# An encoder trunk of two layers: GpSimd's tensor work goes to VectorE, with wider table products and another interleaving

## Chip, cores and metric

The kernel runs on one core of a Trainium2 chip. The metric is the device time of one execution in microseconds (us). The core has five engines that run their own queues of instructions in order: PE (TensorE, matrix products), DVE (VectorE), ACT (ScalarE), POOL (GpSimd) and SP (SyncE, which only issues transfers here). SBUF is the working memory, PSUM the memory that PE writes.

## What is computed

Two layers over 512 tokens of width 1024, all in float32. Each layer is a mixer with two halves, an output projection, a layer norm, an MLP and a second layer norm:

```
h = layer_norm(x)
for each layer:
    proj = h @ w_in                       # z 1024 | x, B, C 2048 | dt 32 | u 1024
    xbc  = silu(depthwise_conv(xbc, 5 taps))
    y_ssd = rms_norm((scan_forward + scan_backward + D * x) * silu(z))    # 16 heads, 4 groups, chunks of 128
    y5 = Re(C s) + d * u                  # S5: 64 groups, complex diagonal state, forward and backward scans
    y_s5 = rms_norm(g * sigmoid(g @ w_glu + b)),  g = gelu(y5)
    h = layer_norm(alpha * h + concat(y_ssd, y_s5) @ w_out)
    h = layer_norm(alpha * h + relu(h @ w1)**2 @ w2)
```

## The kernel before

**Matrix products.** Every float32 product is made of three products of a faster type: a weight tile `raw` is split into `whi` (a rounded copy, ACT, L98) and `wlo` = `raw` - `whi` (L99), the activations likewise, and `mm3` (L105 to L111) adds hi*hi, hi*lo and lo*hi. `proj_tile` (L123) gives 128 output channels for 512 tokens in 24 matmuls; `rows_proj` (L678) gives rows of tokens. The input projection has 32 such tiles in a layer (16 for x, B and C, named `xbc_ps`; 8 `u_ps`; 8 `z_ps`), the GLU 8 (`glu_ps`), the first MLP matrix 32 (`up_ps`); the output projections and the second MLP matrix are `rp`, of which the SSD half of the output projection is the first in a layer.

**The SSD half** (`ssd_group`, L566). For each group: two convolved tiles (`conv_tile`, L539: four taps on DVE, one of them in some tiles on ACT and POOL), B in rows, the products `CB`. For each pair of heads: the chunk states (`xd` L592, `S` L604), and for each head two scans `E2` and `E` (L620, L621), a weight `w` (eight ACT copies, L626 and L627, and a sum L628), the product `E` (L630) and two products `eb` (L631, L632), then the matmuls into `y_ps`.

**The S5 half** (`s5_stream`, L761) works in chunks of 8 tokens. u goes through DRAM (`Ud`). An input table for each of 8 batches and both directions (`s5_vtab`, L372; the tile `Wv` from the loaded `Pv` and `Bv`, six products and sums of 128x512 a direction, L385 to L387) feeds the matmuls `v_ps`, which fill `XV`. Then comes a recurrence of 62 steps over the chunks (`s5_scan`, L408, the tiles `sc`): four DVE instructions for each of two independent parts of 64 columns, L419, L420, L422 and L424, where L422 needs L420, L424 needs L422, and the next step needs L424. Then come output tables (`s5_wtab`, L426; the tile `Wy`, six instructions of 128x512 a direction, L461 to L463, and six small ones of 128x128 for `cp`), the small kernel `kk` that goes to DRAM (`KKd`) and comes back as `Gt`, and the outputs `y`, which are transposed into the GLU's input. For layer 0 the tables are made inside its mixer. For layer 1 they are made during the MLP of layer 0 (`s5_tables`, L491, a generator) and stored in DRAM.

**The MLP** (`mlp_up`, L896). For each `up_ps` tile: ACT takes Relu into `hr` (L903), POOL squares it (L904), ACT copies the rounded half `ahi` (L907), DVE subtracts for `alo` (L908). After each of the first 24 tiles a digit of the string `gen` says how many pieces of `s5_tables` are put into the program.

**What sets the order.** The program is written in one order, in which the lists `mrg` say how many pieces of `s5_stream` stand before each piece of `ssd_group`. A scheduler then reorders instructions on each engine by its own estimate of time and by priorities; the splits always have a raised one, and a table `po` shifts that of named pieces (`scan`, `w`, `v`, `z`, `dt`). Strings of letters (`wu`, `wx`, `wz`, `em`, `yz`, `ct`, `v0`, `v1`, `w0`, `w1`, `gv0` to `gw1`, `glu`, `ln0`) choose DVE (V), POOL (G) or ACT (S) for each instruction that several engines can do. Numbers of buffers limit how far loads and producers run ahead: `Bv` has one, `up_ps` two PSUM banks, `Wy` four (two batches).

Of the kernel before, what the change touches and what calls it, by code (L numbers as in the profile page):

```python
# [1037 lines left out]
```

## Time and profile before

| | before |
|---|---|
| time, median of 3 runs | 2099.39 us (2098.39 to 2099.54) |
| span of the profiled execution | 2094.1 us |
| PE busy | 1754.4 us (84%) |
| DVE busy | 1418.6 us (68%) |
| POOL busy | 837.1 us (40%) |
| ACT busy | 725.5 us (35%) |
| mean granted TensorE clock | 0.914 of full speed |

The profile is of one execution. Its span runs from the first to the last instruction; its own time is not listed apart from the span, and the median of the runs is 5.3 us above it, which is what lies around the span. Stages by the trace: layer 0's mixer to about 637 us, its GLU and projections to 729 us, its MLP to about 1197 us, layer 1's mixer to about 1638 us, its GLU and projections to 1730 us, its MLP to the end.

### The profile page before, as it was taken

To read this page: it belongs to the slowest core of one execution; us is meant where nothing else is said; L and a number is where in the kernel's file an instruction comes from. 1 tells how busy PE (TensorE), PEld (TensorE's weight loads), DVE (VectorE), ACT (ScalarE), POOL (GpSimd) and SP (SyncE) were. 2 spreads that over 40 slices of the span, in tenths; PEclk is the share of its full clock that TensorE was granted. 3 is DMA by queue.
4 is the path that set the end of the run, shared out by engine and by line. 5 is a ranking of instruction groups with operands and counts; after the bars stand their busy time and mean duration, and the time that the engine had idled before them with its cause. 6 is when DMAs were issued, how large, how long until landed. Compare 5 with 4: busy or idle time off the path is not lost.

```text
span 2094.1 us, 28322 instructions
## 1 busy us (share of the span) xinstructions
PE 1754.4 (84%) x10872; PEld 1427.8 (68%) x10872; DVE 1418.6 (68%) x2449; ACT 725.5 (35%) x1156; POOL 837.1 (40%) x557
## 2 busy tenths in 40 slices
PE   3677766676799995967899998776799999999998
PEld 3556555564578883745688887655677888888886
DVE  7468999999956767598733636999963564333335
ACT  2224433354215331211223336244563434232231
POOL 4456755445431128688702234344341112021121
PEclk8779887887799997979899999897999999999999
DMA  4655533434353355656533477542587233323232
GB/s 172 174 149 139 138 96 93 121 83 125 87 177 103 99 123 171 197 161 190 172 102 92 139 225 215 138 119 86 143 215 246 92 110 91 100 91 101 83 108 81
DMA packets 131239, 279.94 MB, mean 134 GB/s; under 512 B 12320, under 2 KB 58400, under 8 KB 130464
## 3 DMA queue, kind: packets, MB, share of 16 engines
q1 hardware_dynamic: 114144, 252.05, 41.8%
q10 hardware_dynamic: 16960, 26.09, 3.6%
q8 instruction: 85, 1.39, 0.3%
q14 instruction: 50, 0.41, 0.1%
HBM read 241.26 MB, written 36.83 MB: 133 GB/s over the span
## 4 chain that ended last, share of the span: by engine, by line
PE 44%; DVE 34%; DMA 9%; POOL 6%; issue 4%; ACT 1%; SPq 1%; POOLq 0%; DVEq 0%; ACTq 0%
PE rp L110 7%; PE rp L111 7%; PE rp L109 7%; PE up_ps L110 4%; PE up_ps L109 4%; PE up_ps L111 4%; DVE sc L422 4%; DVE XV L424 4%; DVE sc L420 4%; DVE sc L419 3%; DMA cb<-in_cb 3%; DMA Bv<-in_bb 2%; DVE E L620 2%; DVE E L621 1%; PE y L519 1%
## 5 line engine op out<-in xcount | busy, mean ns | idle before, releaser
L98 ACT ACTIVATE whi<-raw 128x1024 fp32r<-128x1024 f32 x224 | 236.2, 1057 | 494.9 <-PE rp L111 117.0
L99 DVE TENSOR_TENSOR wlo<-raw,whi 128x1024 fp32r<-128x1024 f32 x166 | 226.3, 1365 | 246.1 <-ACT whi L98 245.6
L904 POOL TENSOR_TENSOR hr<-hr 128x512 f32<-128x512 f32 x64 | 103.2, 1614 | 375.7 <-ACT hr L903 375.7
L99 POOL TENSOR_TENSOR wlo<-raw,whi 128x1024 fp32r<-128x1024 f32 x58 | 142.5, 2459 | 194.1 <-ACT whi L98 187.5
L109 PE MATMUL up_ps<-hThi,whi 128*128 128x512 f32 (+1 forms) x560 | 209.3, 376 | 3.5 <-ACT hr L903 3.2
L110 PE MATMUL up_ps<-hTlo,whi 128*128 128x512 f32 (+1 forms) x560 | 209.5, 375 | 0.1
L111 PE MATMUL up_ps<-hThi,wlo 128*128 128x512 f32 (+1 forms) x560 | 209.2, 374 | 0.0
L110 PE MATMUL rp<-wlo,ahi 128*128 128x512 f32 x448 | 184.0, 411 | 21.3 <-DVE wlo L99 21.3
L109 PE MATMUL rp<-whi,ahi 128*128 128x512 f32 x448 | 174.1, 410 | 21.5 <-ACT whi L98 13.1
L111 PE MATMUL rp<-whi,alo 128*128 128x512 f32 x448 | 182.8, 408 | 0.0
L109 PE MATMUL xbc_ps<-hThi,whi 128*128 128x512 f32 x256 | 113.6, 444 | 41.1 <-ACT z L649 23.6
L109 PEld LDWEIGHTS up_ps<-hThi,whi 128*128 128x128 f32 x560 | 105.9, 190 | 23.9 <-ACT hr L903 4.3
L111 PEld LDWEIGHTS up_ps<-hThi,wlo 128*128 128x128 f32 x560 | 106.4, 190 | 19.1 <-issue 0.4
L110 PEld LDWEIGHTS rp<-wlo,ahi 128*128 128x128 f32 x448 | 88.5, 197 | 44.8 <-DVE wlo L99 23.6
L110 PEld LDWEIGHTS up_ps<-hTlo,whi 128*128 128x128 f32 x560 | 106.3, 190 | 18.6 <-DVE hTlo L175 0.3
L109 PEld LDWEIGHTS rp<-whi,ahi 128*128 128x128 f32 x448 | 87.5, 196 | 43.8 <-ACT whi L98 14.4
L111 PE MATMUL xbc_ps<-hThi,wlo 128*128 128x512 f32 x256 | 111.2, 434 | 1.7 <-POOL wlo L99 1.7
L110 PE MATMUL xbc_ps<-hTlo,whi 128*128 128x512 f32 x256 | 111.4, 435 | 0.0
L908 DVE TENSOR_TENSOR alo<-hr,ahi 128x512 fp32r<-128x512 f32 x64 | 53.6, 839 | 76.6 <-ACT ahi L907 76.3
L111 PEld LDWEIGHTS rp<-whi,alo 128*128 128x128 f32 x448 | 88.3, 197 | 22.2
L422 DVE TENSOR_TENSOR sc<-sc,XV 128x64 f32<-128x64 f32 x248 | 101.9, 429 | 1.9
L420 DVE TENSOR_TENSOR sc<-XV,l 128x64 f32<-128x64 f32 x248 | 101.9, 411 | 0.0
(287 smaller groups left out, 4414.0 us busy)
## 6 DMA issues: line engine op xcount, KB each, us to landing
raw<-in_w SPq DMA_DIRECT2D x128, 512.0 KB
raw<-in_wi SPq DMA_DIRECT2D x64, 512.0 KB
Pv<-pd SPq DMA_DIRECT2D x32, 512.0 KB
ab<-ad SPq DMA_DIRECT2D x32, 512.0 KB
eb<-ad SPq DMA_DIRECT2D x32, 512.0 KB
raw<-in_wo SPq DMA_DIRECT2D x32, 512.0 KB
Bv<-in_bb SPq DMA_DIRECT2D x16, 512.0 KB
U<-Ud SPq DMA_DIRECT2D x128, 64.0 KB
```

What stands on the lines that cost most here:

```text
L98: S.activation(hi, raw, AF.Copy)
L99: e.tensor_tensor(lo, raw, hi.bitcast(F32), op=ALU.subtract)
L109: PE.matmul(o, lhsT=sh, rhs=mh, start=first, stop=False)
L110: PE.matmul(o, lhsT=sh, rhs=ml, start=False, stop=False)
L111: PE.matmul(o, lhsT=sl, rhs=mh, start=False, stop=last)
L419: V.tensor_tensor(t2[i], x[:, ::-1, hs[i]], l8[:, 1, :, hs[i]], op=ALU.mult)
L420: V.tensor_tensor(t1[i], x[:, :, hs[i]], l8[:, 0, :, hs[i]], op=ALU.mult)
L422: V.tensor_tensor(t1[i], t1[i], x1[:, :, hs[i]], op=ALU.add)
L424: V.tensor_tensor(x1[:, :, hs[i]], t1[i], t2[i], op=ALU.add)
L620: V.tensor_tensor_scan(E2, ab[:, 0], C("md"), NEG, op0=ALU.add, op1=ALU.max)
L904: G.tensor_tensor(r, r, r, op=ALU.mult)
L908: V.tensor_tensor(hl, r, hh.bitcast(F32), op=ALU.subtract)
```

## The change

Every tensor operation of POOL is now on DVE; POOL keeps the powers of -0.5 (L150, L673 before), which are one column or four wide. The strings that chose engines are gone. The input table of a direction is made by three instructions of 128x1024 where there were six of 128x512, for which ACT makes a negated copy of `Bv`; the output table likewise, from a copy `pw2` of the powers and a `cp` with a third part. The recurrence runs in one part of 128 columns. In the MLP ACT squares the Relu's result into `ahi` directly, and DVE computes max(`up_ps`, 0) * `hr` from PSUM. `xd` is read from PSUM instead of from the copied row. The `eb` loads take only the 384 columns in use. Fewer buffers for tables, other numbers in `mrg` and `gen`, other priorities.

```
-    wu=["GGGGGGGG", "VGGVGGGG"], wx=["GGGGGGGGGGGGGGGG", "GGGGGGGGGVGVGVGV"], wz=["GVGGGGGG", "GGGVGGGG"],
...
-    v1="GG", w0="VG", w1="GV", gv0="VG", gv1="GG", gw0="GV", gw1="VG", vb=(4, 2), gvb=(4, 3), cbb=2, wyb=4, raw=2,
-    whi=3, wlo=3, nb=dict(mm=3, ss=1, sm=2, s5=2), po=[{}, {"scan": -150, "w": -35}], glu="VVVVGVVV", ln0="SVSG",
-    sn=[2, 2], gen="110211101100201101103101",
+    vb=(3, 2), gvb=(3, 2), cbb=2, wyb=4, raw=2, whi=3, wlo=3, nb=dict(mm=3, ss=1, sm=2, s5=2),
+    po=[{"dt": 60, "scan": 300, "z": 30, "v": 60}, {"scan": -30, "w": -150}], sn=[1, 1], gen="110101122100001130301100",
...
-    def split(hi, lo, raw, e):
+    def split(hi, lo, raw):
         with tc.high_priority():
             S.activation(hi, raw, AF.Copy)
-            e.tensor_tensor(lo, raw, hi.bitcast(F32), op=ALU.subtract)
+            V.tensor_tensor(lo, raw, hi.bitcast(F32), op=ALU.subtract)
...
+        S.activation(B[:, 0], B[:, 2], AF.Copy, scale=-1.0)
...
-            for ri, e in enumerate((e0, e1)[dd]):
-                t1 = pool.tile([128, 512], F32, tag="tv%d" % (e is G), name="tv", bufs=1)
-                e.tensor_tensor(v4(W[:, ri]), P[:, :, 0], v4(B[:, ri]), op=ALU.mult)
-                e.tensor_tensor(v4(t1), P[:, :, 1], v4(B[:, 1 - ri]), op=ALU.mult)
-                e.tensor_tensor(W[:, ri], W[:, ri], t1, op=ALU.add if ri else ALU.subtract)
+            t1 = pool.tile([128, 2, 512], F32, tag="tv", name="tv", bufs=1)
+            pb = lambda r: P[:, :, r].unsqueeze(1).to_broadcast([128, 2, 4, 128])
+            V.tensor_tensor(v4(W), pb(0), v4(B[:, 1:3]), op=ALU.mult)
+            V.tensor_tensor(v4(t1), pb(1), v4(B[:, 0:2]), op=ALU.mult)
+            V.tensor_tensor(W, W, t1, op=ALU.add)
...
-            for ri, e in enumerate((e0, e1)[dd]):
-                t1 = pool.tile([128, 4, 8, 16], F32, tag="tw%d" % (e is G), name="tw", bufs=1)
-                e.tensor_tensor(w[:, ri], cpb(ri), pb(0), op=ALU.mult)
-                e.tensor_tensor(t1, cpb(1 - ri), pb(1), op=ALU.mult)
-                e.tensor_tensor(w[:, ri], w[:, ri], t1, op=ALU.subtract if ri else ALU.add)
+            V.tensor_tensor(wv, cpb(0), pb(0), op=ALU.mult)
+            V.tensor_tensor(t, cpb(1), pb(1), op=ALU.mult)
+            V.tensor_tensor(wv, wv, t, op=ALU.add)
...
-                G.tensor_tensor(xd, X[:, c0:c0 + 3].rearrange("p c (h q) -> p c h q", h=2),
+                V.tensor_tensor(xd, Xp[:, c0:c0 + 3].rearrange("p c (h q) -> p c h q", h=2),
...
-                G.tensor_tensor(w, w, w2, op=ALU.add)
+                V.tensor_tensor(w, w, w2, op=ALU.add)
...
-                G.tensor_tensor(eb[:, 0, 128:512], CT[:, 128:512], eb[:, 0, 128:512], op=ALU.mult)
-                G.tensor_tensor(eb[:, 1, 0:384], CT[:, 0:384], eb[:, 1, 0:384], op=ALU.mult)
+                V.tensor_tensor(eb[:, 0], CT[:, 128:512], eb[:, 0], op=ALU.mult)
+                V.tensor_tensor(eb[:, 1], CT[:, 0:384], eb[:, 1], op=ALU.mult)
...
                     S.activation(r, o, AF.Relu)
-                    G.tensor_tensor(r, r, r, op=ALU.mult)
...
-                    S.activation(hh, r, AF.Copy)
+                    S.activation(hh, r, AF.Square)
+                    V.scalar_tensor_tensor(r, o, 0.0, r, op0=ALU.max, op1=ALU.mult)
                     V.tensor_tensor(hl, r, hh.bitcast(F32), op=ALU.subtract)
```

The order of the instructions moves at many places. Two of them follow. The first is DVE's queue at the end of layer 0's mixer; `sc` and `XV` are the recurrence, `Wy` and `tw` the output tables, and `h_... <- rp` the four results of the first half of the SSD output projection. Before:

```order
L424 TENSOR_TENSOR XV<-sc_2901,sc_2903 128x2x16x2
L99 TENSOR_TENSOR wlo<-raw,whi 128x1024 x2
L461 TENSOR_TENSOR Wy<-cp,pw 128x512 x2
L463 TENSOR_TENSOR Wy<-Wy,tw 128x512
L672 TENSOR_SCALAR r_ssd<-rms_ps 128x4
L462 TENSOR_TENSOR tw<-cp,pw 128x512
L463 TENSOR_TENSOR Wy<-Wy,tw 128x512
L99 TENSOR_TENSOR wlo<-raw,whi 128x1024
L462 TENSOR_TENSOR tw<-cp,pw 128x512
L851 SCALAR_TENSOR_TENSOR h_4588<-rp_4941,r_ssd,h_4588 128x512
```

and now:

```order
L666 TENSOR_SCALAR r_ssd<-rms_ps 128x4
L417 TENSOR_TENSOR XV<-sc_1990,sc_1991 128x64x2
L412 TENSOR_TENSOR sc_2051<-XV,l_287 128x128
L413 TENSOR_TENSOR sc_2050<-XV,l_287 128x128
L415 TENSOR_TENSOR sc_2050<-sc_2050,XV 128x128
L845 SCALAR_TENSOR_TENSOR h_4257<-rp_4469,r_ssd,h_4257 128x512
L845 SCALAR_TENSOR_TENSOR h_4258<-rp_4470,r_ssd,h_4258 128x512
L417 TENSOR_TENSOR XV<-sc_2050,sc_2051 128x64x2
L845 SCALAR_TENSOR_TENSOR h_4259<-rp_4471,r_ssd,h_4259 128x512
```

Before, the recurrence of layer 0 is over when the SSD projection's first results come, and the last output tables stand beside them. Now 22 of the 62 steps stand behind the first of these results and 10 behind the last of all eight, and the output tables of six of the eight batches come after the recurrence. In layer 1 the recurrence now ends at the last of the eight results.

The second place is the MLP of layer 0. POOL's queue before (`hr` the squares, `Wv` and `tv`, `Wy` and `tw` the tables of layer 1):

```order
L904 TENSOR_TENSOR hr<-hr 128x512
L387 TENSOR_TENSOR Wv<-Wv,tv 128x512
L461 TENSOR_TENSOR Wy<-cp,pw 128x512
L462 TENSOR_TENSOR tw<-cp,pw 128x512
L461 TENSOR_TENSOR Wy<-cp,pw 128x512
L463 TENSOR_TENSOR Wy<-Wy,tw 128x512
L904 TENSOR_TENSOR hr<-hr 128x512
```

and DVE's queue now, where the tables, the square (`hr<-up_ps,hr`) and the splits stand in one line:

```order
L902 TENSOR_TENSOR alo<-hr,ahi 128x512
L378 TENSOR_TENSOR Wv<-Pv,Bv 128x1024
L379 TENSOR_TENSOR tv<-Pv,Bv 128x1024
L378 TENSOR_TENSOR Wv<-Pv,Bv 128x1024
L380 TENSOR_TENSOR Wv<-Wv,tv 128x1024
L93 TENSOR_TENSOR wlo<-raw,whi 128x1024
L435 TENSOR_TENSOR tc_6463<-cb,co 128x128
L436 TENSOR_TENSOR tc_6464<-cb,co 128x128
L901 SCALAR_TENSOR_TENSOR hr<-up_ps,hr 128x512
```

The square has moved from POOL to DVE, and up to seven other DVE instructions stand between one tile's `alo` and the next tile's square. POOL's whole queue now holds 24 small powers and the fills at the start and before each layer.

## Rows read from the trace of the kernel before

**Rows 1.** The page's first part, busy time, share and instructions by engine.

```profile
span 2094.1 us, 28322 instructions
PE 1754.4 (84%) x10872; PEld 1427.8 (68%) x10872; DVE 1418.6 (68%) x2449; ACT 725.5 (35%) x1156; POOL 837.1 (40%) x557
```

**Rows 2.** Windows: stretch, its length, busy time of five engines, granted clock, DMA share, GB/s.

```profile
55.00:188.00 133.00, 87.43 (x688) 70.03 (x688) 77.59 (x82) 39.15 (x71) 81.11 (x48) 0.81 0.61 158
188.00:460.00 272.00, 192.72 (x1239) 155.49 (x1239) 265.01 (x574) 102.08 (x187) 140.80 (x94) 0.83 0.42 109
460.00:594.00 134.00, 95.50 (x910) 73.26 (x906) 122.50 (x225) 51.69 (x92) 73.36 (x56) 0.82 0.42 127
...
760.00:1045.00 285.00, 218.22 (x1296) 170.41 (x1295) 211.35 (x198) 56.67 (x83) 215.86 (x138) 0.87 0.59 176
...
1200.00:1325.00 125.00, 111.69 (x1110) 94.94 (x1108) 73.23 (x163) 56.68 (x101) 49.15 (x30) 0.98 0.71 211
1325.00:1540.00 215.00, 162.09 (x969) 132.05 (x970) 208.72 (x538) 104.08 (x190) 87.02 (x64) 0.87 0.50 134
1540.00:1595.00 55.00, 52.96 (x548) 42.14 (x548) 19.30 (x30) 27.96 (x47) 20.14 (x18) 0.94 0.82 229
...
1750.00:2088.00 338.00, 335.64 (x1460) 273.65 (x1458) 129.83 (x150) 96.47 (x123) 52.48 (x34) 1.00 0.31 95
```

**Rows 3.** Timeline of POOL at 193 us: start, length, instruction, idle before it.

```profile
193.67 2.40 POOL L99 TENSOR_TENSOR wlo<-raw,whi 128x1024 fp32r<-128x1024 f32 x1 [6.46 <-ACT whi L98]
```

**Rows 4.** Timeline of DVE from 192 to 194 us.

```profile
192.19 0.27 DVE L419 TENSOR_TENSOR sc<-XV,l 128x64 f32<-128x64 f32 x1
192.37 0.26 DVE L420 TENSOR_TENSOR sc<-XV,l 128x64 f32<-128x64 f32 x1
192.66 0.28 DVE L422 TENSOR_TENSOR sc<-sc,XV 128x64 f32<-128x64 f32 x1
...
193.29 0.27 DVE L419 TENSOR_TENSOR sc<-XV,l 128x64 f32<-128x64 f32 x1
...
193.78 2.42 DVE L422 TENSOR_TENSOR sc<-sc,XV 128x64 f32<-128x64 f32 x1
```

**Rows 5.** The tile xbc: count, shortest, median and longest ns, first and last start.

```profile
L546 DVE SCALAR_TENSOR_TENSOR xbc<-xbc_ps,sp,xbc x32: 724/739/750, 130.4 to 1555.3; 128x511 f32<-128x511 f32 x32
```

**Rows 6.** Timeline of DVE at three places without POOL beside it.

```profile
235.73 0.68 DVE L385 TENSOR_TENSOR Wv<-Pv,Bv 128x512 f32<-128x512 f32 x1
236.33 0.68 DVE L386 TENSOR_TENSOR tv<-Pv,Bv 128x512 f32<-128x512 f32 x1
...
1352.37 1.22 DVE L99 TENSOR_TENSOR wlo<-raw,whi 128x1024 fp32r<-128x1024 f32 x1
1353.50 0.26 DVE L422 TENSOR_TENSOR sc<-sc,XV 128x64 f32<-128x64 f32 x1
...
1378.68 1.22 DVE L620 TENSOR_TENSOR_SCAN E<-ab,cst 128x512 f32<-128x512 f32 x1
```

**Rows 7.** Groups by line and shape, 0 to 600 us: busy, mean ns, idle before.

```profile
L424 DVE TENSOR_TENSOR XV<-sc,sc 128x64 f32<-128x64 f32 x124 | 55.8, 470 | 1.2
...
L620 DVE TENSOR_TENSOR_SCAN E<-ab,cst 128x512 f32<-128x512 f32 x16 | 25.9, 1616 | 1.2 <-DMA ab<-ad 1.2
...
L385 DVE TENSOR_TENSOR Wv<-Pv,Bv 128x512 f32<-128x512 f32 x16 | 20.0, 1256 | 34.2 <-DMA Bv<-in_bb 25.6 <-DMA Pv<-pd 8.6
...
L99 POOL TENSOR_TENSOR wlo<-raw,whi 128x1024 fp32r<-128x1024 f32 x31 | 76.9, 2483 | 86.6 <-ACT whi L98 84.6 <-DVE xbc L547 2.0
```

**Rows 8.** The same for 1197 to 1540 us.

```profile
L422 DVE TENSOR_TENSOR sc<-sc,XV 128x64 f32<-128x64 f32 x124 | 47.8, 408 | 0.8
...
L99 POOL TENSOR_TENSOR wlo<-raw,whi 128x1024 fp32r<-128x1024 f32 x23 | 56.1, 2438 | 81.8 <-ACT whi L98 77.2 <-DMA U<-Ud 4.6
```

**Rows 9.** Timeline of ACT: the first GLU result of layer 0 and of layer 1.

```profile
643.28 0.69 ACT L872 ACTIVATE sg<-glu_ps,sp 128x512 f32<-128x512 f32 x1 [3.54 <-PE glu_ps L111]
...
1645.75 0.69 ACT L872 ACTIVATE sg<-glu_ps,sp 128x512 f32<-128x512 f32 x1
```

More of the change, by code (lines that the diff above doesn't have):

```diff
@@ L128, in proj_tile, with proj_halves @@
         return o
-    def proj_halves(srcs, act, tag, name, es):
-        ws = [wunit(x, e) for x, e in zip(srcs, es)]
+    def proj_halves(srcs, act, tag, name):
+        ws = [wunit(x) for x in srcs]
         os_ = [psum(tag[i % len(tag)], name) for i in range(len(srcs))]
@@ L237, in params @@
         S.activation(cs, r, AF.Sin)
[L239 removed]
+        pw = pool.tile([128, 2, 2, 9, 32], F32, tag="pp_pw", name="pw", bufs=1)
         V.memset(pw[:, 0, :, 0, :], 1.0)
@@ L256, in params @@
             V.tensor_tensor(o[:, 1], ta[:, 1, :, 0:m], tb_[:, 1, :, 0:m], op=ALU.add)
+        pw2 = per.tile([128, 2, 2, 8, 8, 8], F32, tag="pw2", name="pw2", bufs=1)
+        for ri in range(2):
+            for dd in range(2):
+                for x in range(2):
+                    S.activation(pw2[:, ri, dd, :, :, 4 * x:4 * x + 4],
+                                 pw[:, ri, dd, 1:9].rearrange("p k (m q) -> p k m q", q=4), AF.Copy)
         pd = dr.tile([2, 8, 32, 2, 128], F32, tag="pd", name="pd", bufs=2)
@@ L294, in params @@
         V.tensor_tensor(co[:, 1], co[:, 1], den, op=ALU.mult)
-        return dict(P=P_, A=Acol, pw=pw, l8=l8, co=co, pd=pd)
+        return dict(P=P_, A=Acol, pw2=pw2, l8=l8, co=co, pd=pd)
     def dt_prep(l, pool, hT, prm):
@@ L615, in ssd_group @@
                 ab = pool.tile([128, 2, T], F32, tag="ab", name="ab", bufs=1)
-                eb = pool.tile([128, 2, T], F32, tag="eb", name="eb", bufs=2)
-                for i, x in enumerate((ab, eb)):
-                    nc.sync.dma_start(x,
-                                      dtp["ad"][:, hh, i].rearrange("d c s -> d (c s)").unsqueeze(0).to_broadcast([128, 2, T]))
+                eb = pool.tile([128, 2, 384], F32, tag="eb", name="eb", bufs=2)
+                nc.sync.dma_start(ab, dtp["ad"][:, hh, 0].rearrange("d c s -> d (c s)").unsqueeze(0).to_broadcast(
+                    [128, 2, T]))
+                for dd in range(2):
+                    nc.sync.dma_start(eb[:, dd], dtp["ad"][dd, hh, 1, 1 - dd:4 - dd].rearrange(
+                        "c s -> (c s)").unsqueeze(0).to_broadcast([128, 384]))
                 V.tensor_tensor_scan(E2, ab[:, 0], C("md"), NEG, op0=ALU.add, op1=ALU.max)
@@ L662, in rms_add @@
         if k == 0:
-            G.tensor_copy(ssq, sq)
+            V.tensor_copy(ssq, sq)
         else:
-            G.tensor_tensor(ssq, ssq, sq, op=ALU.add)
+            V.tensor_tensor(ssq, ssq, sq, op=ALU.add)
     def rms_end(ssq, name):
@@ L757 @@
         G.memset(XV[:, :, :, 0::127], 0.0)
-        os_ = proj_halves([A["wi"][l, 16 + m] for m in range(3)], act, ["mm"], "u_ps", ens(KN["wu"][l]))
+        os_ = proj_halves([A["wi"][l, 16 + m] for m in range(3)], act, ["mm"], "u_ps")
         with pool_("dt%d" % l) as pool:
@@ L897, in mlp_up @@
                 if q == 0:
-                    os_ = proj_halves([A["w1"][l, m] for m in range(3)], act, ["s5", "s5", "mm"], "up_ps", [V] * 3)
+                    os_ = proj_halves([A["w1"][l, m] for m in range(3)], act, ["s5", "s5", "mm"], "up_ps")
                 hid = []
```

102 lines of the change are left out of this document (43 added, 59 removed), and 4 rows, old and new, of the table mrg.

## The prediction

> **What bounds the kernel now.** I read the busy times first [rows 1]: PE leads with 1754.4 us, DVE has 1418.6 and POOL 837.1 of 2094.1. These are averages over unlike stages, so I went to the windows by stage [rows 2]. In the MLP of layer 1 (1750 to 2088 us) PE is busy for 335.6 of 338 us at full clock; nothing on DVE or POOL can shorten that. The same holds for the GLU and the projections of both layers. In layer 0's mixer the picture turns: from 188 to 460 us DVE is busy for 265 of 272 us, from 460 to 594 for 122.5 of 134, PE for seven tenths and at a clock of 0.83. From 1325 to 1540 us, layer 1's mixer, DVE has 208.7 of 215. From 760 to 1045 us, the MLP in which the next layer's tables are made, POOL has 215.9 and DVE 211.4 of 285, and PE 218.2 at 0.87. So three stages can give time: two mixers that DVE bounds and one MLP that waits for DVE and POOL in turn.
>
> The third view is the timeline, read for why DVE is so busy. An instruction of the recurrence on 64 columns takes 0.27 us; the same instruction at 193.78 us takes 2.42 us [rows 4], and POOL began a `wlo` of 2.40 us at 193.67 [rows 3]: they end 0.13 us apart. A DVE instruction with two SBUF operands stands still while POOL works on SBUF. One that reads PSUM does not: the 32 convolution taps of L546 lie between 724 and 750 ns wherever they stand [rows 5]. The group means show how much of DVE's busy time is such waiting: 470 ns for the 124 instructions of L424 in layer 0 and 1256 ns for L385 [rows 7], where free ones take 260 to 280 ns [rows 4] and 680 ns [rows 6].
>
> **The change part by part.** Prices first, from start to start of free neighbours: 0.60 us for two SBUF operands of 512 columns, 1.13 us for 1024 [rows 6], so 1.035 ns a column; hence 0.47 for 384 columns. A recurrence instruction of 64 columns takes 0.18 us behind an independent one [rows 4], so one of 128 takes 0.18 + 0.066 = 0.246.
>
> *Layer 0's mixer, stretch removed.* The four recurrence groups, of which one is shown [rows 7], hold 218 us in 496 instructions; free they are 496 x 0.26 = 129: 89 us. The six table groups, one shown [rows 7], hold 104 us in 93 instructions, free 93 x 0.68 = 63: 41. The two scans of each head, 32 instructions with 25.9 [rows 7] and 24.4 us, take 1.22 us free [rows 6]: 11. The smaller groups (coefficients, `E`, splits): 16. Together 157 us.
>
> *Added to DVE there.* 31 `wlo` [rows 7] x 1.13 = 35; POOL's 93 table instructions, which become half as many of twice the width, 93 x 0.565 = 53; 16 sums `w` x 0.60 = 10; 32 `eb` and 16 `xd` x 0.47 = 23; 16 others (`E`, gate, taps, sums of squares) x 0.62 = 10. Together 131 us.
>
> *Saved by width.* The recurrence: 62 x (8 x 0.18 - 4 x 0.246) = 28; DVE's own tables 93 x (0.60 - 0.565) = 3. So DVE needs 157 + 31 - 131 = 57 us less.
>
> *What is late next.* Before, the tables end at 600 us, where the stretch of rows 7 ends, and the first GLU result comes at 643.3 [rows 9]; between them PE still has some 90 of the SSD projection's 192 matmuls to do, 20 us at the 338 us in which layer 1's MLP does 1536 [rows 2]. Now the projection stands ahead of the outputs, under the recurrence's tail: 20 us off the end. Against that, `Wy` has room for two batches, so the third must wait for the first output, which needs the last step: 5 us. And ten steps stand behind the projection with nothing between them. A dependent pair starts 0.29 us apart and a step of 64 columns 1.10 [rows 4], so a step of 128 alone takes 1.10 + 4 x 0.066 = 1.36 and not 0.98: 4 us. DVE's 55 idle us from 55 to 188 [rows 2] are mostly waits for `Bv` and `Pv` (34 us at L385 [rows 7]). `Bv` has one buffer, and POOL, whose table instructions also queue behind `wlo` of 2.48 us [rows 7], gives it back late. I take 15 of the 55, between none and all. Layer 0: -57 - 20 - 15 + 5 + 4 = -83, with ends of -40 (the 57 less some 17 for waits that the rows don't show) and -130 (all 55 idle us gone).
>
> The VectorE page of the Trainium skill ("VectorE: DVE Perf Modes", The DRAIN you can't avoid) says that a chain of VectorE instructions pays the same gap with or without semaphores. By that the ten steps would lose nothing and the sum would be 4 us lower; the starts in the rows above show the dependent pair later, so I go by them.
>
> *Layer 0's MLP.* PE's 218.2 us at 0.87 are 190 at full clock, so at most 95 of the 285 us [rows 2] can go. The square leaves POOL, whose queue put it behind tables; ACT's square costs what its copy cost. DVE gets one instruction of about 0.74 us from PSUM [rows 5] for each tile. A piece of tables now takes DVE 6 x 1.13 = 6.8 us, or 8.5 with the seven small ones. In the first quarter DVE has 7 x 6.8, 8 tiles x (1.13 + 0.60 + 0.74), 14 us for the second matrix and about 70 small instructions x 0.26 for the parameters: 100 us, against PE's 84, a quarter of 338. In the third, 8 x 8.5 + 34 = 102. So 16 + 18 us stay lost, of which the second quarter takes 9 back, and I add 5 for waits at single tiles: -65, with ends of -30 and -95.
>
> The change adds a wait here: the PSUM bank of an `up_ps` tile was free after ACT's Relu and is now free after DVE's square. Behind that waits PE, two tiles on. I cost it at nothing, since a second bank covers one tile of about 5 us. With that cover gone, 24 tiles would lose 6.8 - 5.3 each, 36 us; that lies inside the ends.
>
> *Layer 1's mixer.* There are no tables. Stretch: the recurrence, one group shown [rows 8], 184 us - 129 = 55, scans and others 13. Added: 23 `wlo` [rows 8] x 1.13 = 26, `w`, `eb`, `xd` and others 37. Width: -28. DVE alone would end 33 us earlier, at 1507. PE may not follow. Its work from 1200 to 1595 is 112 x 0.98 + 162 x 0.87 + 53 x 0.94 = 300 us at full clock [rows 2]; the SSD projection's 41 come in, and the 320 output matmuls go behind (31 us at 53.0 us for 548 records [rows 2]). That makes 310. At a share of 0.93, between 0.89 and 0.96 in the first and the last of these stretches, it ends at 1533. Then come 31 us of outputs and 14 us for the last GELU, transposes, splits and the first GLU tile: 1578, where it was 1645.8 [rows 9]. That is -68, with ends of -33 (DVE's part alone) and -91 (PE without a gap).
>
> *At nothing:* the negated `Bv`, the copy `pw2` and the ACT square, since ACT has 35% [rows 1]; the layer norms' DVE form; the shorter `eb` loads; the sums of squares in the GLU stage, where PE bounds. If ACT were late, each of the 16 `Bv` copies would cost a table 0.6 us, 10 us in all.
>
> **Sum.** -83 - 65 - 68 = -216: a span of 2094.1 - 216 = 1878 us. The median of the runs lies 5.3 us over the span, so **1883 us**. The ends add up to -103 and -316: 1996 and 1783.
>
> **Rivals.**
> *The S5 tail lies bare* (chance 0.17). All six late output tables of layer 0 follow one another with the trip of `kk` through DRAM unhidden, 15 us more for each batch, a little more than the 9 us of one table: +90, so 1973 us. For it: the tail now stands behind the SSD half with no other work of PE beside it. Against it: `Wy` has four buffers, so a table can run beside the trip of the one before.
> *PE without gaps* (0.08). All upper ends hold and the clock stays at full: 1788 us. Against it: no mixer stretch shows it.
> *The stretch is not POOL's doing* (0.05), but that of transfers or of access patterns. Then 131 - 31 us are added in layer 0, 63 - 28 in layer 1, and DVE in layer 0's MLP gets 21 + 68 on top of 211 of 285, +15: 2099 + 150 = 2249 us, slower. It decides from where less than 6 tenths of the stretch goes away (100 of 157, 35 of 68). Against it stand the two instructions that end together at 196 us, and the taps from PSUM that are never stretched.
>
> The Trainium skill ("Perfetto Trace Analysis", Optimizing Scalar/DVE Operations) says that with a saturated VectorE it may make sense to move work to ScalarE or even GPSIMD, which speaks for the kernel before; by it this change would cost the 131 and 63 us that DVE takes on. The same paragraph warns of the read port that the two share, and the rows above bear the warning out.
>
> That the change does not do what it says is out: POOL's queue holds 24 small powers and a few fills.
>
> **How the numbers follow.** The forecast has 0.68, the three rivals 0.17, 0.08 and 0.05; 0.02 is left for no difference (within 0.2%, about what a measurement of this kernel can tell). Faster: 0.68 + 0.17 + 0.08 = 0.93; slower 0.05. The range of 1800 to 1990 us holds the forecast's ends nearly whole and the first rival.
>
> **What would show it.** Right: L424's successor at about 0.33 us for 128 columns and no two-operand instruction over 1.3 us; DVE's sum between 1230 and 1330 us in place of 1418.6; layer 0's first GLU result near 560, its MLP about 65 us shorter, layer 1's first GLU result 68 us nearer to the start of its mixer. Wrong: single stretched instructions without POOL; DVE idle before `Wy` between two batches; PE waiting for `hr` in layer 0's MLP; a clock that stays at 0.83 in the mixers.

## The result, and where the time went

Four runs of the changed kernel have a median of 2031.57 us (2027.98 to 2032.78), those of the kernel before beside them 2098.89: a ratio of 0.9689 (95% interval 0.9668 to 0.9710). It is faster by 67 us; the prediction said 1883 us, with a range from 1800 to 1990. The profiled execution has a span of 2029.3 us where the one before had 2094.1 [rows 1].

The first part of the page of the changed kernel answers to [rows 1]:

```profile
span 2029.3 us, 27508 instructions
PE 1738.4 (86%) x10872; PEld 1416.0 (70%) x10872; DVE 1342.7 (66%) x2300; ACT 728.1 (36%) x1175; POOL 33.6 (2%) x31
```

POOL is nearly empty, and VectorE's sum fell by 76 us although it took on POOL's work: the stretch is gone, as said, though 1342.7 is still 13 us over the top of what the prediction gave as a sign of being right (1230 to 1330). The time by stage, each boundary the first matmul of its kind in the trace, shows what did not follow (the last column is a run of the experiments, taken up there):

| stage, us | before | after | forecast change | measured | moved_only |
|---|---|---|---|---|---|
| start to layer 0's first GLU matmul | 637.0 | 621.8 | -83 | -15 | 595.3 |
| GLU and projections | 91.9 | 92.6 | 0 | +1 | 92.6 |
| layer 0's MLP, to layer 1's first `u` tile | 465.0 | 406.2 | -65 | -59 | 397.4 |
| layer 1's mixer, to its first GLU matmul | 444.0 | 451.2 | -68 | +7 | 431.1 |
| the rest | 456.3 | 457.6 | 0 | +1 | 459.9 |

The MLP came out as forecast; both mixers did not. The windows of the changed kernel, columns as in [rows 2], show where in them:

```profile
188.00:460.00 272.00, 204.88 (x1255) 168.62 (x1254) 243.30 (x479) 139.04 (x258) 0.00 (x0) 0.86 0.44 116
460.00:512.00 52.00, 30.01 (x125) 24.17 (x123) 47.64 (x115) 7.64 (x7) 1.05 (x1) 0.80 0.37 122
512.00:622.00 110.00, 74.72 (x1053) 55.99 (x1054) 50.16 (x70) 12.74 (x30) 0.00 (x0) 0.78 0.35 90
714.00:1120.00 406.00, 384.66 (x2159) 309.64 (x2158) 290.97 (x437) 123.97 (x181) 5.35 (x4) 0.97 0.54 169
...
1320.00:1490.00 170.00, 135.41 (x697) 111.69 (x696) 159.04 (x344) 86.63 (x153) 1.14 (x1) 0.91 0.39 118
1490.00:1572.00 82.00, 57.61 (x665) 43.51 (x666) 2.42 (x5) 10.29 (x18) 0.00 (x0) 0.82 0.72 188
```

Up to 512 us VectorE is busy for 243 of 272 and for 48 of 52 us, and then, for 110 us, no engine bounds: PE is busy for 75 of them, VectorE for 50, at a granted clock of 0.78. In layer 1 the same from 1490 to 1572: VectorE, busy for 159 of the 170 us before, has 2.4 of 82. These are the output tails of S5. What begins them stands in the timelines of VectorE and PE of the changed kernel (start, length, instruction, idle before it):

```profile
509.62 0.38 DVE L415 TENSOR_TENSOR sc<-sc,XV 128x128 f32<-128x128 f32 x1
510.03 0.37 DVE L417 TENSOR_TENSOR XV<-sc,sc 128x128 f32<-128x128 f32 x1
510.44 0.37 DVE L412 TENSOR_TENSOR sc<-XV,l 128x128 f32<-128x128 f32 x1
510.73 0.36 DVE L413 TENSOR_TENSOR sc<-XV,l 128x128 f32<-128x128 f32 x1
511.12 0.37 DVE L415 TENSOR_TENSOR sc<-sc,XV 128x128 f32<-128x128 f32 x1
511.53 0.37 DVE L417 TENSOR_TENSOR XV<-sc,sc 128x128 f32<-128x128 f32 x1
```

```profile
493.36 0.39 PE L105 MATMUL rp<-whi,hTlo 128*128 128x512 f32 x1
512.05 1.97 PE L515 MATMUL y<-Wy,XV 64*64 64x128 f32 x16 [18.30 <-DVE XV L417]
```

PE stands for 18.3 us and starts the first output when the last step of the recurrence has ended. In the kernel before, PE and VectorE stood like this:

```profile
457.80 1.09 PE L519 MATMUL y<-Wy,XV 64*64 64x128 f32 x16
```

```profile
577.58 1.35 DVE L424 TENSOR_TENSOR XV<-sc,sc 128x64 f32<-128x64 f32 x1
```

The first output ran 121 us **ahead** of the last step. With two parts, batches 0 to 3 need only the first part, which led by far; four of eight batches were through by 548 us, under the second part's steps, and three of layer 1's ahead of its last step at 1536. One part of all eight batches takes that away. The first GLU results, to be held against [rows 9] (the prediction had the one of layer 0 near 560 us), in ScalarE's timeline of the changed kernel:

```profile
632.92 0.69 ACT L866 ACTIVATE sg<-glu_ps,sp 128x512 f32<-128x512 f32 x1
...
1582.85 0.69 ACT L866 ACTIVATE sg<-glu_ps,sp 128x512 f32<-128x512 f32 x1
```

### The profile page after: what moved, and what is told of

It reads as the page before. It is cut to its first block, busy times and chain, and to the rows that moved or that the text cites. A ratio compares the mean times of both kernels' runs of the same rounds, so it can differ in the third digit from the quotient of the medians.

```text
span 2029.3 us, 27508 instructions
## 1 busy us (share of the span) xinstructions
PE 1738.4 (86%) x10872; PEld 1416.0 (70%) x10872; DVE 1342.7 (66%) x2300; ACT 728.1 (36%) x1175; POOL 33.6 (2%) x31
## 4 chain that ended last, share of the span: by engine, by line
PE 47%; DVE 24%; DMA 20%; issue 4%; ACT 3%; SPq 2%; POOLq 0%; POOL 0%; ACTq 0%; DVEq 0%
PE rp L103 6%; PE rp L105 6%; PE rp L104 6%; PE up_ps L103 5%; PE up_ps L104 5%; PE up_ps L105 5%; DMA ab<-ad 5%; DMA Bv<-in_bb 4%; DVE wlo L93 3%; PE y L515 3%; DMA Vd<-Wv 2%; PE glu_ps L103 1%; DMA raw<-in_wi 1%; PE glu_ps L104 1%; PE glu_ps L105 1%
## 5 line engine op out<-in xcount | busy, mean ns | idle before, releaser
L93 DVE TENSOR_TENSOR wlo<-raw,whi 128x1024 fp32r<-128x1024 f32 x224 | 273.7, 1222 | 280.6 <-ACT whi L92 280.5
L104 PE MATMUL rp<-wlo,ahi 128*128 128x512 f32 x448 | 178.7, 399 | 2.9 <-DVE wlo L93 2.9
L103 PE MATMUL rp<-whi,ahi 128*128 128x512 f32 x448 | 166.1, 400 | 3.8 <-ACT whi L92 3.7
L515 PE MATMUL y<-Wy,XV 64*64 64x128 f32 x1024 | 86.6, 317 | 23.0 <-DVE XV L417 23.0
L104 PE MATMUL xbc_ps<-hTlo,whi 128*128 128x512 f32 x256 | 105.4, 412 | 0.0
L105 PE MATMUL xbc_ps<-hThi,wlo 128*128 128x512 f32 x256 | 104.9, 410 | 0.0
L515 PEld LDWEIGHTS y<-Wy,XV 64*64 64x64 f32 x1024 | 68.2, 158 | 37.6 <-issue 37.6
L378 DVE TENSOR_TENSOR Wv<-Pv,Bv 128x1024 f32<-128x1024 f32 x32 | 39.0, 1222 | 59.9 <-DMA Bv<-in_bb 20.6
L859 DVE TENSOR_TENSOR alo<-gF,ahi 128x512 fp32r<-128x512 f32 x16 | 9.8, 686 | 99.7 <-ACT ahi L858 99.7
L911 DVE TENSOR_TENSOR h<-h,rp 128x512 f32<-128x512 f32 x64 | 43.5, 683 | 48.6 <-PE rp L105 48.6
## 6 DMA issues: line engine op xcount, KB each, us to landing
raw<-in_w SPq DMA_DIRECT2D x128, 512.0 KB
raw<-in_wi SPq DMA_DIRECT2D x64, 512.0 KB
Pv<-pd SPq DMA_DIRECT2D x32, 512.0 KB
ab<-ad SPq DMA_DIRECT2D x32, 512.0 KB
raw<-in_wo SPq DMA_DIRECT2D x32, 512.0 KB
Bv<-in_bb SPq DMA_DIRECT2D x16, 512.0 KB
```

The source lines that it names most:

```text
L93: V.tensor_tensor(lo, raw, hi.bitcast(F32), op=ALU.subtract)
L103: PE.matmul(o, lhsT=sh, rhs=mh, start=first, stop=False)
L104: PE.matmul(o, lhsT=sh, rhs=ml, start=False, stop=False)
L105: PE.matmul(o, lhsT=sl, rhs=mh, start=False, stop=last)
L378: V.tensor_tensor(v4(W), pb(0), v4(B[:, 1:3]), op=ALU.mult)
L515: PE.matmul(yv[64 * a:64 * a + 64, q], lhsT=XV[64 * a:64 * a + 64, ri, 4 * m + q, 64 * dd:64 * dd + 64], rhs=W[dd][64 * a:64 * a + 64, ri, ...
```

## The experiments

Seven theories: **A**, the one part holds all outputs back; **B**, the new interleaving put the tail behind the SSD half; **C**, the chain of one wide part is what is long; **D**, loads pace the tail because their buffers come free late; **E**, they pace it because `cb` stands late in SyncE's queue; **R**, the tail is a ring of buffers; **S**, the stretch is GpSimd's doing. Each kernel was run four to six times, wy2 once; ratios are to the kernel before, run on the same chip. Layer 0's first GLU matmul came 6 us earlier in tail_bufs than in the changed kernel although nothing differs up to there, so single stages are read to about 6 us.

| kernel | median us | ratio (95%) |
|---|---|---|
| changed kernel | 2031.57 | 0.9689 (0.9668-0.9710) |
| old_order | 2043.27 | 0.9753 (0.9722-0.9783) |
| two_parts | 2000.31 | 0.9547 (0.9511-0.9582) |
| halves | 2029.34 | 0.9691 (0.9650-0.9731) |
| tail_bufs | 2023.42 | 0.9649 (0.9622-0.9677) |
| wlo_pool | 2046.16 | 0.9759 (0.9708-0.9810) |
| cb_queue | 2029.67 | 0.9674 (0.9630-0.9719) |
| before_one | 2116.94 | 1.0098 (1.0064-1.0132) |
| combo | 1999.88 | 0.9534 (0.9487-0.9582) |
| lead28 | 1979.38 | 0.9456 (0.9413-0.9499) |
| lead44 | 2009.03 | 0.9600 (0.9566-0.9634) |
| sq_pool | 2026.24 | 0.9677 (0.9644-0.9711) |
| narrow | 2023.80 | 0.9661 (0.9622-0.9699) |
| wy6 | 2029.35 | 0.9687 (0.9662-0.9713) |
| tab_pool | 2078.64 | 0.9904 (0.9869-0.9939) |
| best | 1993.70 | 0.9516 (0.9485-0.9548) |
| moved_only | 1979.95 | 0.9435 (0.9406-0.9463) |
| lead28_bufs | 1976.63 | 0.9411 (0.9382-0.9440) |
| wy2 (one run) | 2128.96 | not compared |

Layer 0's marks in the traces, us; the fourth column is the third less the first:

| kernel | first output | last step | first GLU matmul | output to GLU |
|---|---|---|---|---|
| before | 457.8 | 578.9 | 637.0 | 179 |
| before_one | 522.4 | 521.1 | 641.4 | 119 |
| changed | 512.0 | 511.9 | 621.8 | 110 |
| two_parts | 497.1 | 502.5 | 607.7 | 111 |
| halves | 468.6 | 573.0 | 620.8 | 152 |
| lead28 | 479.7 | 534.1 | 594.8 | 115 |
| lead44 | 470.7 | 553.3 | 601.9 | 131 |
| moved_only | 486.7 | 503.8 | 595.3 | 109 |
| narrow | 511.3 | 511.1 | 613.4 | 102 |
| wy6 | 514.9 | 514.7 | 602.2 | 87 |
| wy2 | 490.4 | 490.3 | 673.3 | 183 |

**One part or the order of the pieces?** before_one changes one number of the kernel before, old_order puts the old tables of numbers into the changed kernel:

```diff
-    sn=[2, 2], gen="110211101100201101103101",
+    sn=[1, 1], gen="110211101100201101103101",
```

> The kernel before with nothing but the recurrence in one part instead of two. Theory A (one part holds back the outputs of the first four batches, which in the kernel before ran from 458 to 546 us, ahead of the last step at 579): layer 0's time from the last step to the first GLU result grows from 58 to 90 to 110 us, as does layer 1's by some 20; against that stand 248 instructions less in each layer: 2085 to 2135 us. If the split does not matter for the outputs, VectorE's 28 us per layer and the stretch that goes with these instructions come off: 2020 to 2050 us.

> The changed kernel with the tables of the interleaving (mrg, po, gen) of the kernel before; the recurrence stays in one part. Theory A (one part: no output of any batch can start before the last step of the recurrence of all eight, so all outputs and six late tables stand bare behind it): the recurrence stands at the same places of VectorE's queue as in the changed kernel, so nothing changes: 2031 us, within 10, layer 0's first GLU result still about 110 us after the last step of the recurrence. Theory B (the new interleaving put the S5 tail behind the SSD half): undoing it gives back 60 to 100 us, 1930 to 1970 us.

before_one decides for A. The recurrence of layer 0 ends 58 us earlier than in the kernel before, and the first GLU matmul comes 4 us later, because the first output starts after that end and no longer 121 us ahead of it: from the last step to the GLU it is 120 us and not 58, even more than the 90 to 110 expected. In all it is slower by 1.0%. PE's and VectorE's timelines of before_one:

```profile
521.55 0.95 PE L670 MATMUL rms_ps<-cst,ssq 128*128 128x1 f32 x8
522.43 0.76 PE L519 MATMUL y<-Wy,XV 64*64 64x128 f32 x10
```

```profile
520.76 0.38 DVE L424 TENSOR_TENSOR XV<-sc,sc 128x128 f32<-128x128 f32 x1
```

old_order is no faster but 12 us slower, and its layer 0 has the same marks within 4 us (516 and 623). B falls.

**The recurrence in two parts again.** two_parts is the changed kernel with `sn=[2, 2]`. halves lets both parts share scratch tiles and emits all steps of the first before those of the second. lead28 and lead44 emit the second part 28 or 44 steps late:

```diff
-            for k in range(1, 63, 2):
+            lead = 28
+            for s in range(1, 63 + lead):
                 with prio("scan"):
-                    s5_scan(per, prm, XV, k, k + 2, KN["sn"][l])
-                yield
+                    if s < 63:
+                        s5_step(per, prm, XV, s, 0)
+                    if s > lead:
+                        s5_step(per, prm, XV, s - lead, 1)
+                if s % 3 == 0:
+                    yield
```

> The changed kernel with the recurrence in two parts (batches 0 to 3 and 4 to 7), the program's pieces in the same order. The order of the queue has both parts side by side to the end (about five steps apart), so theory A expects no early outputs, only VectorE's 28 us more per layer and an earlier start: 2030 to 2075 us. Theory C (what cost the time is the longer dependent chain of the one wide part): two chains fill each other's gaps, so 15 to 40 us faster.

> The changed kernel with the recurrence in two parts that are made to run one after the other (they share their scratch tiles): batches 0 to 3 are through before 4 to 7 begin. Theory A: the first four outputs of each layer come some 80 us before the last step, the bare tail is halved (layer 0 from 110 to about 55 us, layer 1 from 82 to about 40), VectorE pays 28 us more per layer and some lone steps at the end (15 x 1.1 us), so 1990 to 2025 us. Theory B expects no gain and the 28 us twice: 2070 to 2090.

> The changed kernel with the recurrence in two parts of which the second starts 28 steps behind the first (two scratch tiles, shared in turn). Theory A (the bare tail begins when the first four batches have their last step, and lasts 105 to 110 us in layer 0 and 66 to 82 in layer 1 from there): VectorE's queue has the first part's last step some 100 instructions earlier than in two_parts, about 15 to 30 us in each layer, and the second part has run out before its outputs are wanted: 1950 to 1980 us. If only the chain's gaps mattered (theory C), it is no faster than two_parts: 1998 to 2015 us.

> The same with a lead of 44 steps. Theory A: the first part ends earlier still (in layer 0 by 66 instructions, in layer 1 by 72, some 10 to 15 us each), but some 44 steps of the second part at 1.1 to 1.7 us then stand beside the first outputs, and from a certain lead they are what is waited for: 1940 to 1990 us, within 15 us of lead28. Theory C: 2000 to 2020 us.

two_parts won 1.4%, where A alone expected nothing: VectorE is busy for 319 us in layer 1's mixer in place of 304, and yet layer 0's first output comes 15 us earlier and layer 1's 23. The first step is at 164 us and not at 239, since the first part waits for four batches of input tables and not for eight. That the two chains also fill each other's gaps, as C has it, fits, but was not separated from this. halves shows both sides of A: the first output 43 us earlier than in the changed kernel, 48 us from the last step to the GLU instead of 110, but a last step 61 us later; together nothing, less than I had expected. lead28 lies between, and it pays, within what A expected and below what C did (1998 to 2015): the first output 17 us ahead of two_parts', and the second part's steps, to 534 us, hidden beside the first four batches. With lead44 the second part is waited for, and the time is 19 us over what A allowed it. In the six kernels of the table with four `Wy` in which no second part is waited for (before, halves and lead44 left out) it is 102 to 119 us from the first output to the GLU: the tail has a length of its own, and what moves is its start.

**What paces the tail?** VectorE's waits in the changed kernel from 512 to 622 us (us in all, times, longest):

```profile
DVE tc L435 <- DMA cb<-in_cb: 20.5, 4, 7.9
DVE alo L859 <- ACT ahi L858: 20.1, 1, 20.1
DVE kk L473 <- PE kk_ps L470: 9.2, 6, 3.2
DVE Wy L457 <- PE y L515: 9.2, 2, 6.6
```

cb_queue issues `cb` from GpSimd's queue; tail_bufs gives layer 1 two `U`, two `gst` and three `Gt`; wy6 makes room for six `Wy` (it is narrow, below, with half of `pw2` and `tw`, and one `cp` instead of two); wy2 has room for two, and `AHEAD = 0`:

```diff
-        nc.sync.dma_start(cb_, A["cb"][l, m])
+        nc.gpsimd.dma_start(cb_, A["cb"][l, m])
...
-        U = s5_loadU(sy, Ud, k // 2, 1)
+        U = s5_loadU(sy, Ud, k // 2, 1 + l)
...
-    vb=(3, 2), gvb=(3, 2), cbb=2, wyb=4, raw=2, whi=3, wlo=3, nb=dict(mm=3, ss=1, sm=2, s5=2),
+    vb=(3, 2), gvb=(3, 2), cbb=2, wyb=6, raw=2, whi=3, wlo=3, nb=dict(mm=3, ss=1, sm=2, s5=2),
```

> The changed kernel with the load of the table coefficients cb issued from GpSimd's queue instead of SyncE's, where it stands behind the U and Gt loads. Theory E (layer 0's bare tail of 110 us is paced by this queue: VectorE waited 20.5 us for cb in four of its six late batches): the tail falls to about 90 us, 2008 to 2018 us in all. If the round of outputs and kk trips sets the pace anyway, 2027 to 2034 us.

> The changed kernel with more buffers for layer 1's output tail alone: U and gst two instead of one, Gt three instead of two (layer 0 has no room). Theory D (the bare tail is paced by the trips through DRAM: each pair of batches waits for its U and Gt loads, which wait for the buffers of the pair before): layer 1's tail from the last step to the first GLU result goes from 82 to 50 to 65 us, 2000 to 2015 us. If TensorE at its low clock sets the pace, it stays within 5 us: 2027 to 2033.

> The kernel narrow (2023.8 us) with room for three batches of output tables (six Wy) instead of two; the room comes from the undoubled pw2, a half tw and one cp. Theory R (the tail is a ring: table, kk through DRAM and back, output, buffer free, some 26 us round, two batches in it, so 13 us per batch): three in the ring come to 9 to 10.5 us per batch, VectorE's own 9.7, and one more table is done ahead of the last step: layer 0's tail from the first output to the first GLU result 80 to 95 us instead of 102 to 110, the recurrence 5 to 9 us later: 2005 to 2018 us. If the tail is the bare sum of the work on TensorE at its low clock, it stays within 5 us of narrow.

> The changed kernel with room for one batch of output tables (two Wy) and no table ahead of its output. Theory R: one batch in the ring, 22 to 26 us for each: layer 0's tail of 110 us grows to 165 to 200. If two batches never overlapped, it stays at 110 to 130 (one more table behind the last step).

E falls: in cb_queue VectorE waits less for `cb` but more for `Wy` (29.7 us for both before, 30.5 now), and the tail stayed at 110 us.

```profile
DVE Wy L457 <- PE y L515: 17.1, 4, 7.6
DVE tc L435 <- DMA cb<-in_cb: 13.4, 4, 3.9
```

What D is worth is not clear of noise: tail_bufs is 8 us lower (0.4%), with overlapping intervals, and 6 of the 8 lie ahead of layer 0's GLU, where the two kernels do not differ. Layer 1's time from the last step to the GLU went from 81 to 74 us, where D expected 50 to 65. PE waited there 19.8 us for `Gt`, `Gd` and `U` from 1490 to 1572 us; with the buffers it waits for `Wy` instead:

```profile
PE y L515 <- DMA Wy<-Wd: 13.5, 5, 5.9
```

R holds in layer 0. Eight batches take 183 us with one in the ring, 110 (102 in narrow) with two and 87 with three: 22.9, 13.7 and 10.9 us each. Times the batches in the ring that is a round of 23, 27 and 33 us, so the round itself lengthens and each place added brings less. What closes the ring is read in the waits of wy2, from 505 to 700 us: each table waits for the output before it, and each output for its `kk` to come back from DRAM.

```profile
DVE Wy L457 <- PE y L515: 79.3, 6, 16.5
...
PE y L510 <- DMA Gt<-KKd: 69.1, 7, 11.1
```

But wy6 as a whole is no faster than narrow, against what R expected: the 11 us won at the first GLU matmul go again in the MLP (426 us for 417) and in layer 1's mixer (451 for 443), where I have no cause for either; its smaller `tw` and its one `cp` were not tried alone. Of wy2, with its one run, only the tail is read.

**The stretch and the MLP.** wlo_pool puts `e = G` into the splits of the mixers; narrow has the table products at 512 columns; tab_pool is narrow with POOL's old share of the products in layer 0's MLP; sq_pool has the square of both MLPs on POOL again:

```diff
+                    G.tensor_tensor(r, r, r, op=ALU.mult)
...
-                    S.activation(hh, r, AF.Square)
-                    V.scalar_tensor_tensor(r, o, 0.0, r, op0=ALU.max, op1=ALU.mult)
+                    S.activation(hh, r, AF.Copy)
```

> The changed kernel with the 32 weight splits (wlo) of each mixer back on GpSimd; all else stays on VectorE. Theory S (a VectorE instruction with two SBUF operands stands still while GpSimd works on SBUF): VectorE gives up 64 x 1.13 = 72 us and gets 64 stretches of 1.2 to 2.4 us, 77 to 154 us; its sum comes to 1340 to 1425 us, single instructions of the recurrence take 2 us and more, taps from PSUM stay at 0.74; 2030 to 2070 us in all. If the stretch of the kernel before was not GpSimd's doing, VectorE is 36 us lighter in each mixer and the time falls to 1960 to 1990 us.

> The kernel narrow with five of eight table products of the first layer's MLP put on GpSimd in the old pattern; the mixers stay as they are. If the tables' place won the 58 us of this MLP: its time from the first up tile to the last product returns from 373 to 410 to 430 us, 2060 to 2080 us in all, and VectorE's remaining two-operand instructions there are stretched to 2 us and more. If the MLP's gain came from elsewhere (order of the pieces): within 10 us of narrow.

> The changed kernel with all table products at the old width of 512 (twice as many instructions, on VectorE). By the rows of the kernel before a pair costs 0.07 us more than one of 1024 columns: 96 more instructions in layer 0's mixer and 96 in its MLP, 3 to 7 us each: 2035 to 2045 us. If width is worth more, as it was for the recurrence: 2050 to 2065 us.

> The changed kernel with the square of the MLP back on GpSimd (64 instructions, read back by ScalarE's copy), as before the change. If the square was what held the first layer's MLP (the view of the prediction), that MLP gives back 15 to 40 of the 58 us it won: 2045 to 2075 us. If the tables' move and the end of the stretch won them, VectorE loses 0.74 us for each tile and the time stays within 10 us: 2021 to 2041.

The tile `sc` (count, shortest, median and longest ns, first and last start), first in the changed kernel, then in wlo_pool:

```profile
L415 DVE TENSOR_TENSOR sc<-sc,XV x62: 350/382/403, 235.8 to 511.1; 128x128 f32<-128x128 f32 x62
```

```profile
L415 DVE TENSOR_TENSOR sc<-sc,XV x62: 348/380/2431, 237.8 to 507.1; 128x128 f32<-128x128 f32 x62
```

Without POOL no instruction of the recurrence is over 0.41 us; with its 29 splits in layer 0 some take 2.4. VectorE gave up work and its sum still rose, from 1342.7 to 1365.1 us, and the kernel became slower by 15 us (the two intervals just touch). tab_pool shows it by groups, of VectorE in layer 0's MLP, first narrow, then tab_pool:

```profile
L905 DVE SCALAR_TENSOR_TENSOR hr<-up_ps,hr 128x512 f32<-128x512 f32 x32 | 22.0, 691 | 0.3 <-ACT ahi L904 0.3
...
L463 DVE TENSOR_TENSOR Wy<-Wy,tw 128x512 f32<-128x512 f32 x32 | 21.1, 691 | 0.0
```

```profile
L463 DVE TENSOR_TENSOR Wy<-Wy,tw 128x512 f32<-128x512 f32 x16 | 22.1, 1379 | 0.1
L905 DVE SCALAR_TENSOR_TENSOR hr<-up_ps,hr 128x512 f32<-128x512 f32 x32 | 21.8, 684 | 2.9 <-ACT ahi L904 2.9
```

With two SBUF operands 691 becomes 1379 ns: half of the instructions take the time of all. Over this whole MLP VectorE is busy for 322 us in tab_pool and 298 in narrow, although 120 of its 192 table products went to POOL. With PSUM as one source nothing changes. The Trainium skill ("SBUF — State Buffer", Who interferes with whom) says that a VectorE instruction with two SBUF inputs contends with a GpSimd instruction that reads SBUF, for a port pair that is an exclusive lock, and that one with at most one SBUF input, outside the two-port modes, does not contend. By that rule nothing is gained by sharing such work, and both pairs of rows agree. The MLP takes 459 us in tab_pool and 417 in narrow: the tables' place won most of it. The square won little: layer 0's MLP is 11 us longer in sq_pool, but layer 1's mixer is 9 shorter, and the whole is 5 us faster, with overlapping intervals. narrow is no slower either, against both values expected of it, so the wide products bring nothing that the whole time shows.

**What is the move worth without the rest?** moved_only is narrow with `sn=[2, 2]` and the old order. It keeps the small parts of the change (`xd` from PSUM, shorter `eb` loads, fewer buffers), which no run takes apart. combo, best and lead28_bufs add gains up.

> The changed kernel with the recurrence in two parts, the table products at the old width and the interleaving of the kernel before: what is left of the change is the move from GpSimd (and the square on ScalarE). By the single parts: two_parts at 2000 us, 12 for the order (old_order), 0 to 11 for the width in the first layer's MLP: 2005 to 2025 us, so that the move alone is worth 70 to 90 us and the rest of the change took some of it back. If the parts of the change hang together: 2030 us or more.

> The changed kernel with the recurrence in two side-by-side parts, the buffers of tail_bufs in layer 1 and cb from GpSimd's queue. If the three gains add (31 + 8 + the 20 expected of cb): 1965 to 1985 us. If the two-part recurrence and the tail's loads were one and the same gain: 1990 to 2005 us.

> lead28 (1979 us) with the table products at the old width and the buffers of tail_bufs in layer 1. If the gains add (8 of the buffers, 0 to 8 of the width): 1963 to 1975 us. If layer 1's tail is now paced by the second part of the recurrence: 1975 to 1985.

> lead28 with the buffers of tail_bufs in layer 1 (two U, two gst, three Gt). If its output tail still waits for these loads: 1968 to 1976 us; if the second part of the recurrence sets it now: 1977 to 1985.

moved_only takes 5.65% off the kernel before, 118 us, where the whole change takes 3.1%. Its windows, columns as in [rows 2]:

```profile
188.00:460.00 272.00, 216.72 (x1317) 176.17 (x1315) 257.66 (x699) 143.03 (x258) 0.00 (x0) 0.88 0.45 122
...
688.00:1085.00 397.00, 381.79 (x2159) 308.04 (x2158) 297.37 (x534) 123.39 (x180) 5.82 (x4) 0.98 0.55 172
...
1437.00:1516.00 79.00, 69.88 (x641) 54.56 (x640) 14.10 (x17) 14.47 (x22) 1.02 (x1) 0.96 0.79 219
```

So the move from GpSimd, with these small parts, is the gain, and the other parts together took some 50 us of it back. It beats my sum from single parts by 25 us. two_parts differs from it in width and order only, so these cost 20 us beside two parts; which of the two was not run apart. combo (nothing over two_parts) and best (14 us worse than lead28, with intervals that just overlap) point the same way: gains of a few us in one tail do not add. lead28_bufs has the lowest median, but its interval and those of moved_only and lead28 overlap. All three beat both kernels.

## Why the prediction was wrong

- **Stretch removed: right.** See wlo_pool and tab_pool. The rival that denied it is out. A recurrence instruction of 128 columns takes 0.37 us where the prediction had 0.33.
- **VectorE's need in layer 0: right in size; the place of the last step was luck.** VectorE's busy time in this mixer fell by 66 us (526.6 to 460.4) where the sum had 57. With -15 and +4 that puts the last step at 511, and it ended at 511.9. But two misses cancel in it, as the windows up to the last step show, first before, then now:

```profile
0.00:579.00 579.00, 385.44 (x2826) 310.19 (x2827) 497.63 (x983) 207.91 (x368) 312.11 (x211) 0.82 0.46 125
0.00:512.00 512.00, 361.20 (x2352) 297.44 (x2352) 410.39 (x815) 206.84 (x366) 6.68 (x11) 0.84 0.52 138
```

  The idle time did not fall by 15 us but grew from 81 to 102 (from 55 to 188 us, where the 15 were taken from, 51 of the 55 idle us are left). And VectorE has 87 us less to do by then, not 66: 52 us of output tables now come behind the last step, where it was 15, and less of other work is left there.
- **"What is late next": the step that failed.** It let the time from the last step to the GLU shrink from 58 us by 20 and grow by 5. It read the tail before as the whole tail, though four batches' outputs lay ahead of the last step, under the second part, and did not ask which outputs that part's end had released. Behind one last step stand eight outputs and six tables: 110 us and not 43. These 67 us are the miss of layer 0, as the other two cancel.
- **"Saved by width", 28 us a layer: mis-sized.** The sum has instructions of 128 columns 0.246 us apart; at 510.44 and 510.73 two independent ones start 0.29 apart, and with that the same sum gives 62 x (1.44 - 1.16) = 17. VectorE's busy time differs by 6 us in layer 0's mixer (466 in two_parts, 460) and by 15 in layer 1's, first two_parts, then the changed kernel:

```profile
1110.80:1542.70 431.90, 373.93 (x2870) 307.50 (x2869) 319.07 (x869) 199.43 (x351) 2.82 (x3) 0.94 0.59 171
1120.60:1571.70 451.10, 376.56 (x2869) 309.82 (x2868) 304.46 (x620) 198.92 (x351) 2.93 (x3) 0.92 0.57 163
```

  And the narrower form is 31 us faster in all, so its split bought more than its instructions cost.
- **Ten lone steps at 1.36 us:** measured 1.50 (509.62 to 511.12 in the timeline), a small miss. Independent starts are 0.29 us apart, dependent ones 0.39 to 0.41.
- **Layer 0's MLP, -65: right in size,** -59, but little of it by the square, which I named with the tables: sq_pool puts it back for 11 us in this MLP and for nothing in all. The wait for a PSUM bank, costed at nothing, is 8 us in which PE waits for `hr`.
- **Layer 1, -68: wrong twice.** The last step comes 370 us after the mixer's start and not 339 as the sum had it; before it was 343. The sum had PE busy for 0.93 of the time at full clock; from 1126.8 us to the last step it was for 314 of 364 us (0.86), at a clock of 0.94. VectorE's work that stood behind the last step (40 us between 1536 and 1638 in the kernel before) now stands ahead of it, and 2.4 us are left behind; that this is what delays the last step is argued and was not tried alone. Then come 81 us to the first GLU matmul where the sum had 37 (45 to the first GLU result). The 31 us in it were mis-sized: I counted 320 output matmuls of a layer and priced them by records of the trace, but each of them has two records. The rows of the tile `y` in layer 1's tail of the changed kernel (columns as in [rows 5]) have 512 and 120 of the 640 records:

```profile
L515 PE MATMUL y<-Wy,XV x512: 269/269/473, 1490.6 to 1568.4; 64*64 64x128 f32 x171
...
L510 PE MATMUL y<-Gt,U x120: 272/323/476, 1492.5 to 1567.4; 128*64 128x128 f32 x120
```

  At the same price that is 62 us and not 31. The rest goes with waits for loads (19.8 us on PE, above), with nothing beside them, and a granted clock of 0.82.
- **The rival "S5 tail lies bare" was what happened.** Its 15 us per batch were near the 13.7 measured. I gave it 0.17 because "`Wy` has four buffers, so a table can run beside the trip of the one before". That is so, and it makes 13.7 of 22.9, not the 8.5 of a table. I also gave it no cause beyond the projection's new place, and none for layer 1, which put its 1973 us 59 too low.
- **Smaller slips.** By its own terms the far end of layer 0 is -123 and not -130, and that of the rival without gaps is 1783 us and not 1788. The 5.3 us added to the span are too many: in the profiled run of the changed kernel 2.0 us lie around it (2031.33 and 2029.3).

## What to carry to other kernels

Before you merge independent chains to save instructions, list what the end of each releases: here the split cost VectorE 6 and 15 us in the two mixers, and without it the wait from layer 0's last step to the GLU grew by 62 us, more than the 58 by which that step came earlier (before_one). Price a loop through a few buffers as its round trip divided by the batches in it, not by its busiest engine, and let the round grow with them. And where VectorE and GpSimd shut each other out, giving VectorE all of it can cost less than the sharing did: here that, with a few small parts, was worth 118 us.

## What was not expected of the hardware

A tail of short waits pays twice on PE, once for the wait and once for the matmuls behind it. After the 18.3 idle us 16 records of output matmuls took 1.97 us (above, at 512.05); behind a later wait of 2.38 us in the same tail they took 1.97 again, then 1.53 and then 1.09:

```profile
542.08 0.69 PE L510 MATMUL y<-Gt,U 128*64 128x128 f32 x4 [2.38 <-DMA Gd<-gst]
542.70 1.97 PE L515 MATMUL y<-Wy,XV 64*64 64x128 f32 x16
...
545.23 1.53 PE L515 MATMUL y<-Wy,XV 64*64 64x128 f32 x16
546.69 0.44 PE L510 MATMUL y<-Gt,U 128*64 128x128 f32 x4
547.06 1.09 PE L515 MATMUL y<-Wy,XV 64*64 64x128 f32 x16
```

1.97 and 1.09 are the same work at the lower and at the higher of the clock's two levels: the windows of the two stretches at 512.05 and 547.06 (columns as in [rows 2]) have a granted clock of 0.50, which is 1.2 GHz, and of 1.00, 2.4 GHz.

```profile
512.05:514.02 1.97, 1.97 (x18) 1.64 (x20) 0.00 (x0) 0.00 (x0) 0.00 (x0) 0.50 0.03 8
547.06:548.15 1.09, 1.09 (x20) 0.92 (x20) 0.52 (x3) 0.00 (x0) 0.00 (x0) 1.00 0.97 118
```
